# Down projections of two MLPs in 2x2 blocks: seven products instead of eight

## The chip, the cores and the metric

The kernel runs on one core of one Trainium2 chip. The metric is the device time in microseconds, the median of the timed runs.

## The reference

A decoder trunk of two layers over 512 tokens and a width of 1024, all in float32. Layer 0 begins with a mixer of a convolution and a state-space scan, layer 1 with gated linear attention; both go on with cross-attention into 256 memory tokens and an MLP. What bears on this case is the MLP and the layer norm behind it:

```
def sq_relu_mlp(x, w1, w2):          # w1 1024 x 4096, w2 4096 x 1024
    return jnp.square(jax.nn.relu(x @ w1)) @ w2
h = layer_norm(DEEPNORM_ALPHA * h + sq_relu_mlp(h, mlp_w1[i], mlp_w2[i]), ln_g[i, 2], ln_b[i, 2])
```

## The kernel before

**Products.** Every matrix product is made from pairs. `split` (L104, L105) turns a float32 tile into hi, its rounding to float32r, made by ScalarE, and lo, the exact rest, made by VectorE (or by GpSimd where `lo_pat` says "g"). `mm3` (L159 to L161) makes one product from three matmuls, hi x hi, hi x lo and lo x hi, each 128 by 128 by 512 columns. Weights come as blocks of 1 MB (tag "ws", two buffers, issued by SyncE) and are split in `wpair` into tiles of 128 x 1024 (tags "wh" and "wl", six buffers each).

**The MLP.** `mlp` works through the 4096 hidden features in four quarters (`qd`) of 1024. In the up part `feat_tiles` makes 8 tiles of 128 features x 512 tokens, 24 matmuls each, with the activations moving. The evacuation takes relu on ScalarE (L473), the square on VectorE (L475) and splits it at once. In the down part `tok_half` makes 512 output columns for four tiles of 128 tokens, twice; each token tile collects 8 feature tiles, 24 matmuls. VectorE adds the sums to the residual h (L485 in the first quarter, with the factor alpha, L487 after). The last quarter goes through `out_proj`: its second half takes one token tile after the other, so that the layer norm of a tile (statistics L279 and L285, the inverse root on GpSimd L266 and L267, then L290 and L291) and its transposes into the next `xT` (`transpose_in`) stand beside the next tile's matmuls. The norm of the last tile has no matmuls of its own quarter behind it.

**Memory.** Activations of both layers come from one pool of 31 tiles of 128 x 512 (tag "t2"), open from the first cross-attention to the end. PSUM has three tags: "acc" (3 banks), "aux" (3) and "acb" (2); `acc()` deals acc and acb out in turn.

**Order.** The program is written for a tile framework whose planner plays it through with its own costs when it is built, and puts the instructions of each engine in the order in which they come out there. So the order on an engine is not that of the text; but once built it is fixed, and each engine takes its queue in order. Pools limit how far an engine can run ahead. SyncE's loads are one such queue.

Of the kernel before, what the change touches and what calls it, by code (L numbers as in the profile page):

```python
# [8 lines left out]
F32 = mybir.dt.float32  # L9
F32R = mybir.dt.float32r  # L10
AF = mybir.ActivationFunctionType
ALU = mybir.AluOpType
AX = mybir.AxisListType

P = 128
D = 1024
S = 512
NT = S // P
NK = D // P
ML = 256  # L20
FF = 4096
DEPTH = 2
ALPHA = (2 * DEPTH) ** 0.25
# [6 lines left out]
class Trunk:  # L30
# [26 lines left out]

    # issue order only, on one engine
    def after(self, b, a):
# [40 lines left out]

    # hi is src rounded to float32r, lo the exact rest
    def split(self, src, hi, lo, eng=None):
# [3 lines left out]

    # the same from PSUM, without the vector engine
    def split_pool(self, ps, hi, lo):
# [4 lines left out]

# [1 line left out]
    def lo_engine(self):  # L115
# [39 lines left out]

# [1 line left out]
    def mm3(self, out, a, b, start, stop):  # L157
        nc = self.nc
        nc.tensor.matmul(out, a[0], b[0], start=start, stop=False)  # L159
        nc.tensor.matmul(out, a[0], b[1], start=False, stop=False)  # L160
        nc.tensor.matmul(out, a[1], b[0], start=False, stop=stop)  # L161

# [4 lines left out]

    # output features on partitions; the first `halves` tiles begin with the first half of the tokens
    def feat_tiles(self, w, c0, n, xT, evac, halves=0):
# [29 lines left out]

    # output tokens on partitions, 512 columns; xT: list of (hi, lo) by k  # L200
    def tok_half(self, w, r0, c0, xT, evac, t_outer=False, nt=NT, late=None, joint=None):
# [36 lines left out]

# [1 line left out]
    def new_xT(self):  # L240
# [28 lines left out]

# [1 line left out]
    def begin_ln(self, i, j):  # L271
# [23 lines left out]

    # projection back to the residual, then layer norm
    def out_proj(self, w, xT, h, i, j, scaled=False, mid=None):
# [28 lines left out]

# [1 line left out]
    def mem_T(self):  # L328
# [133 lines left out]

# [1 line left out]
    def mlp(self, i, h, xT):  # L464
        nc = self.nc
        w1, w2 = self.aps["mlp_w1"][i], self.aps["mlp_w2"][i]
        NQ = 4
        for qd in range(NQ):
            r2 = []

            def evac(m, ps):
                r = self.t2()
                nc.scalar.activation(r, ps, AF.Relu)  # L473
                sq = self.t2()
                nc.vector.tensor_tensor(sq, r, r, ALU.mult)  # L475
                hi, lo = self.t2(F32R), self.t2(F32R)
                self.split(sq, hi, lo)
                r2.append((hi, lo))
            self.feat_tiles(w1, qd * D, NK, xT, evac, halves=4 if qd == 0 else 0)
            if qd < NQ - 1:  # L480
                for hf in range(2):
                    def ev(t, ps, hf=hf):
                        y = h[t, hf]
                        if qd == 0:
                            nc.vector.scalar_tensor_tensor(y, y, ALPHA, ps, ALU.mult, ALU.add)  # L485
                        else:
                            nc.vector.tensor_tensor(y, y, ps, ALU.add)  # L487
                    self.tok_half(w2, qd * D, hf * S, r2, ev)
            else:
                return self.out_proj(w2[qd * D:(qd + 1) * D, :], r2, h, i, 2, scaled=True)  # L490

# [23 lines left out]
    def run(self):  # L515
        tc = self.tc
        self.kv_dram = [tc.dram_tile([2, 8, P, S], F32, name=f"kvd{i}") for i in range(DEPTH)]
        with tc.tile_pool(name="ep", bufs=8, reuse_waits="tile") as self.ep, self.sbuf_phase(16) as self.tp, \
                self.psum_phase(False) as self.px:
            self.lo_pat = "g"  # L520
            xT = self.load_x(self.aps["even_w_in"][0], D)
            h, xT = self.even(xT, self.x_tiles)
        self.lo_pat = "v"
        with tc.tile_pool(name="rp", bufs=4, reuse_waits="tile") as self.ep, self.sbuf_phase(31) as self.tp, \
                self.psum_phase(True) as self.px:
            h, xT = self.xa(0, h, xT, *self.kv_load(0))
            h, xT = self.mlp(0, h, xT)
            h, xT = self.odd(h, xT)
            h, xT = self.xa(1, h, xT, *self.kv_load(1))
            self.mlp(1, h, xT)  # L530

# [1 line left out]
    def bc(self, ap, n, w):  # L533
# [41 lines left out]

    # x times a [D, 16] weight, transposed: the sum of rows 0..15 and 32..47 of [P, S] in PSUM
    def narrow(self, w, c0, xT):
# [76 lines left out]

    # silu gate times two, from a product in PSUM
    def gate2(self, ps, th):
# [22 lines left out]
    def ssd_chunk(self, g, c, d, xs, BT, CT):  # L679
        nc = self.nc  # L680
        v = nc.vector
        r3 = lambda ap: ap.rearrange("p (h c) -> p h c", c=64)
        sl = slice(c * P, (c + 1) * P)
# [9 lines left out]
        pb = self.aux()  # L693
        nc.tensor.matmul(pb[:, 0:P], BT[:, sl], CT[:, sl], start=True, stop=True)
        cb = self.sp.tile([P, P], F32, tag="cb", bufs=2, name=self.nm("cb"))
        bt, xw = None, None
        if c < 3:
            nc.tensor.transpose(pb[:, P:2 * P], BT[:, sl], self.ident)
            bt = self.sp.tile([P, P], F32, tag="bt", bufs=2, name=self.nm("bt"))
            nc.scalar.copy(bt, pb[:, P:2 * P])  # L700
            xw = self.t2()
            nc.gpsimd.tensor_tensor(r3(xw), r3(xdt), self.bc(d["dte"][:, hs], 8, 64), ALU.mult)
# [4 lines left out]
        for q in range(2):  # L707
# [4 lines left out]
            for j in range(4):  # L712
                h = c * 16 + h0 + j
# [8 lines left out]
    def ssd_out(self, g, c, d, p, xs, CT, H, zs, norm_g):  # L722
        nc = self.nc
        v = nc.vector
        r3 = lambda ap: ap.rearrange("p (h c) -> p h c", c=64)
        sl = slice(c * P, (c + 1) * P)
# [3 lines left out]
        for i in range(8):  # L730
            last = nc.tensor.matmul(py[:, i * 64:(i + 1) * 64], Ms[i // 4][:, (i % 4) * P:(i % 4 + 1) * P],
                                    xdt[:, i * 64:(i + 1) * 64], start=True, stop=True)
# [7 lines left out]
        if c < 3:  # L740
            pst = self.aux()
            with self.tc.issue_after(last.ins):
                nc.tensor.matmul(pst, p["bt"], p["xw"], start=True, stop=True)
            H2 = self.sp.tile([P, S], F32, tag="H", bufs=2, name=self.nm("H"))
            if c == 0:
                nc.scalar.copy(H2, pst)
            else:
                nc.gpsimd.tensor_tensor(r3(H2), r3(H), self.bc(d["cd"][:, hs], 8, 64), ALU.mult)
                v.tensor_tensor(H2, H2, pst, ALU.add)
            H = H2  # L750
# [25 lines left out]

    # one tile of the wide conv, a tap at a time
    def conv_taps(self, u):
# [129 lines left out]

# [1 line left out]
    def odd(self, h, xT):  # L910
# [24 lines left out]

        # 16 x the log gate, summed within chunks of 64
        az, mn, bs = [], [], []
# [210 lines left out]
```

## Time and profile before

| what | value |
|---|---|
| timed runs | 1651.32, 1651.59, 1653.93 us, median 1651.59 |
| span of the profiled execution (its own time is not listed apart) | 1651.3 us |
| TensorE matmuls: busy, share | 1617.0 us, 98% |
| VectorE | 957.9 us, 58% |
| ScalarE | 614.0 us, 37% |
| GpSimd | 363.8 us, 22% |
| mean granted TensorE clock, share of full speed | 0.994 |

The profile is of one execution. Matmul records overlap, since matmuls are pipelined: what one costs is the distance between starts, not the length of its record. The MLP of layer 0 lies at some 553 to 900 us, that of layer 1 from some 1290 us to the end.

### The profile page before, as it was taken

What the parts mean: (1) busy time and instruction counts of PE and PEld (TensorE: products, weight loads), DVE (VectorE), ACT (ScalarE), POOL (GpSimd) and SP (SyncE); (2) the same over time, 40 slices, a digit from 0 to 9 for tenths busy, and PEclk for the clock granted to TensorE, in tenths of its full rate; (3) what the DMA queues carried; (4) which work ended last, traced back from release to release, by engine and by line L of the source; (5) the groups of instructions that cost most, each with busy time, mean ns of one, the idle gap of its engine ahead of it and who ended that gap; (6) DMA issues with size and microseconds to landing.
All of it is one profiled execution on the core that took longest, in us unless ns stands there. A gap on an engine that the chain in (4) does not pass through costs nothing.

```text
span 1651.3 us, 19881 instructions
## 1 busy us (share of the span) xinstructions
PE 1617.0 (98%) x8010; PEld 1353.9 (82%) x8010; DVE 957.9 (58%) x1279; ACT 614.0 (37%) x994; POOL 363.8 (22%) x288
## 2 busy tenths in 40 slices
PE   8998999999999999999999999999999999999998
PEld 7886878788988988888888788897988988888886
DVE  3998999975655634433447644444745734433445
ACT  4355557552442422323232534352332423223230
POOL 4654957744102100000001121222201200000001
PEclk9998999999999999999999999999999999999999
DMA  7224226632711332233232232275311322332221
GB/s 243 95 78 127 87 68 205 216 127 77 255 51 52 128 102 89 90 102 102 85 100 77 103 102 77 77 252 200 125 61 52 128 93 86 102 103 92 87 77 51
DMA packets 134798, 182.72 MB, mean 111 GB/s; under 512 B 6821, under 2 KB 83797, under 8 KB 134706
## 3 DMA queue, kind: packets, MB, share of 16 engines
q1 hardware_dynamic: 134162, 181.26, 33.5%
q8 instruction: 63, 1.03, 0.3%
q0 software_dynamic: 544, 0.20, 0.1%
q14 instruction: 29, 0.24, 0.0%
HBM read 170.92 MB, written 10.52 MB: 110 GB/s over the span
## 4 chain that ended last, share of the span: by engine, by line
PE 79%; DVE 14%; DMA 3%; issue 2%; POOL 1%; ACT 1%; SPq 0%; POOLq 0%; DVEq 0%; ACTq 0%
PE acc L161 16%; PE acc L159 16%; PE acc L160 16%; PE accb L161 9%; PE accb L159 9%; PE accb L160 9%; DVE cv L805 6%; DVE xs L651 1%; DMA ws<-in_odd_w_out_dram 1%; DVE h L291 1%; DMA kvd<-kv 1%; PE aux L253 1%; DVE t L651 1%; PE aux L161 1%; PE aux L159 1%
## 5 line engine op out<-in xcount | busy, mean ns | idle before, releaser
L105 DVE TENSOR_TENSOR wl<-ws,wh 128x1024 fp32r<-128x1024 f32 x216 | 271.7, 1260 | 430.0 <-ACT wh L104 430.0
L104 ACT CAST wh<-ws 128x1024 fp32r<-128x1024 f32 x276 | 288.9, 1050 | 560.5 <-PE acc L161 175.4
L159 PE MATMUL acc<-t,wh 128*128 128x512 f32 (+1 forms) x856 | 309.9, 363 | 6.0 <-DVE h L660 3.8
L161 PE MATMUL acc<-t,wl 128*128 128x512 f32 (+1 forms) x856 | 309.3, 362 | 0.0
L160 PE MATMUL acc<-t,wh 128*128 128x512 f32 (+1 forms) x856 | 309.2, 361 | 0.0
L159 PE MATMUL acc<-wh,t 128*128 128x512 f32 x704 | 279.0, 396 | 2.0 <-ACT kv L111 1.2
L160 PE MATMUL acc<-wl,t 128*128 128x512 f32 x704 | 278.5, 396 | 0.0
L161 PE MATMUL acc<-wh,t 128*128 128x512 f32 x704 | 276.0, 395 | 0.0
L105 POOL TENSOR_TENSOR wl<-ws,wh 128x1024 fp32r<-128x1024 f32 x60 | 151.3, 2531 | 300.0 <-ACT wh L104 299.6
L159 PEld LDWEIGHTS acc<-t,wh 128*128 128x128 f32 x856 | 163.7, 192 | 30.6 <-DVE h L660 4.0
L161 PEld LDWEIGHTS acc<-t,wl 128*128 128x128 f32 x856 | 163.8, 191 | 24.5 <-issue 1.7
L160 PEld LDWEIGHTS acc<-t,wh 128*128 128x128 f32 x856 | 164.0, 192 | 23.9 <-issue 1.0
L159 PEld LDWEIGHTS acc<-wh,t 128*128 128x128 f32 x704 | 132.5, 188 | 32.4 <-ACT kv L111 1.6
L160 PEld LDWEIGHTS acc<-wl,t 128*128 128x128 f32 x704 | 132.6, 188 | 29.9 <-issue 1.2
L161 PEld LDWEIGHTS acc<-wh,t 128*128 128x128 f32 x704 | 132.4, 188 | 29.4 <-issue 0.2
L805 DVE SCALAR_TENSOR_TENSOR cv<-u,cw,cv 128x511 f32<-128x511 f32 (+24 forms) x210 | 145.5, 728 | 0.5
L160 PE MATMUL accb<-wl,t 128*128 128x512 f32 x352 | 139.4, 396 | 0.0
L159 PE MATMUL accb<-wh,t 128*128 128x512 f32 x352 | 138.8, 394 | 0.0
L161 PE MATMUL accb<-wh,t 128*128 128x512 f32 x352 | 138.3, 395 | 0.0
L266 POOL TENSOR_SCALAR s<-s 128x1 f32<-128x1 f32 (+1 forms) x44 | 23.0, 524 | 474.5 <-DVE s L285 438.4
L161 PE MATMUL accb<-t,wl 128*128 128x512 f32 (+1 forms) x344 | 119.1, 346 | 0.0
L160 PE MATMUL accb<-t,wh 128*128 128x512 f32 (+1 forms) x344 | 118.9, 346 | 0.0
(286 smaller groups left out, 2135.5 us busy)
## 6 DMA issues: line engine op xcount, KB each, us to landing
ws<-in_mlp_w_dram SPq DMA_DIRECT2D x64, 1024.0 KB, 5.3
ws<-in_even_w_in_dram SPq DMA_DIRECT2D x17, 1024.0 KB, 5.3
ws<-in_odd_w_in_dram SPq DMA_DIRECT2D x12, 1024.0 KB, 5.1
ws<-in_xa_w_k_dram SPq DMA_DIRECT2D x8, 1024.0 KB, 5.0
ws<-in_xa_w_v_dram SPq DMA_DIRECT2D x8, 1024.0 KB, 6.0
kvd<-kv SPq DMA_DIRECT2D x32, 256.0 KB, 5.1
ws<-in_even_w_out_dram SPq DMA_DIRECT2D x8, 1024.0 KB, 5.2
ws<-in_xa_w_q_dram SPq DMA_DIRECT2D x8, 1024.0 KB, 5.9
```

Of the source, the lines that this page charges most:

```text
L104: self.last_hi = nc.scalar.copy(hi, src)
L105: (eng or nc.vector).tensor_tensor(lo, src, hi.bitcast(F32), ALU.subtract)
L159: nc.tensor.matmul(out, a[0], b[0], start=start, stop=False)
L160: nc.tensor.matmul(out, a[0], b[1], start=False, stop=False)
L161: nc.tensor.matmul(out, a[1], b[0], start=False, stop=stop)
L253: nc.tensor.transpose(ps[:, j * P:(j + 1) * P], halves[hf][:, j * P:(j + 1) * P], self.ident)
L266: nc.gpsimd.tensor_scalar(r, var, scale, eps, op0=ALU.mult, op1=ALU.add)
L291: nc.vector.scalar_tensor_tensor(y, y, r, ln["b"][:, sl], ALU.mult, ALU.add)
L651: nc.vector.scalar_tensor_tensor(c[:, s:], x[:, :S - s], w[:, 3 - s:4 - s], c[:, s:], ALU.mult, ALU.add)
L805: nc.vector.scalar_tensor_tensor(cs[j][:, s:], u[m][:, :S - s], w[:, 30 - s:31 - s], cs[j][:, s:], ALU.mult, ALU.add)
```

## The change

The down projection of each quarter becomes one call of `strassen`. The activations of the quarter (512 tokens x 1024 features) are cut into 2 x 2 blocks of 256 tokens x 512 features, the weights (1024 x 1024) into 2 x 2 blocks of 512 x 512, and the four output blocks come from seven block products, P1 to P7, in Winograd's form. With A11 and A12 the two feature halves of the first 256 tokens (`A1`, `A2` at `t0`), A21 and A22 those of the last 256 (`t1`):

```
P1 = A11 B11              P2 = A12 B21
P3 = (A21 + A22)(B12 - B11)
P4 = (A21 + A22 - A11)(B22 - B12 + B11)
P5 = (A12 - A21 - A22 + A11) B22
P6 = (A11 - A21)(B22 - B12)
P7 = A22 (B22 - B12 + B11 - B21)
```

Each product is 2 token tiles x 4 feature tiles x 3 matmuls. P2 goes on in the banks of P1, P5 in those of P3, P7 in those of P6, after VectorE has read what stood there. P1 + P4 is needed in three output blocks; it is collected in `E` over all four quarters and added once, in the last. Sums and differences of blocks are made by VectorE, in float32, before the split; each of the seven operand pairs is split on its own. The squared activations stay unsplit in tiles of four features ("ab"); the square moves to ScalarE. Two up tiles of the next quarter stand ahead of each call but the last. The layer norm of token tiles 0 and 1 comes with P5, that of tiles 2 and 3 with P7. The down weights get buffers of their own ("sq", four). The pool of activations is opened once per layer and closed before the MLP, which opens its own (`mp`) in the same memory. The scratch memory of DMAs is cut to 4096 bytes, and three tags of the state-space scan change pools. Blank lines and lost comments are left out here.

```
-    def mm3(self, out, a, b, start, stop):
-        nc = self.nc
-        nc.tensor.matmul(out, a[0], b[0], start=start, stop=False)
-        nc.tensor.matmul(out, a[0], b[1], start=False, stop=False)
-        nc.tensor.matmul(out, a[1], b[0], start=False, stop=stop)
+
+
+    def mm3(self, out, a, b, start, stop, more=False):
+        nc = self.nc
+        nc.tensor.matmul(out, a[0], b[0], start=start, stop=False, skip_group_check=more)
+        nc.tensor.matmul(out, a[0], b[1], start=False, stop=False, skip_group_check=more)
+        nc.tensor.matmul(out, a[1], b[0], start=False, stop=stop, skip_group_check=more)
...
+    def blk_load(self, w, r, c):
+        st = self.mp.tile([P, 4, S], F32, tag="sq", bufs=4, name=self.nm("sq"))
+        self.nc.sync.dma_start(st, w[r:r + S, c:c + S].rearrange("(k p) c -> p k c", p=P))
+        return st
+    def blk_w(self, st):
+        r = []
+        for j in range(2):
+            hi, lo = self.wpair(st[:, 2 * j:2 * j + 2, :], (P, 2, S))
+            r += [(hi[:, i, :], lo[:, i, :]) for i in range(2)]
+        return r
+    def blk_a(self, src):
+        hi, lo = [self.mp.tile([P, 4, 256], F32R, tag=t, bufs=3, name=self.nm(t)) for t in ("sh", "sl")]
+        self.split(src, hi, lo)
+        return hi, lo
+    def blk_sub(self, dst, a, b):
+        for j in range(2):
+            ks = slice(2 * j, 2 * j + 2)
+            self.nc.vector.tensor_tensor(dst[:, ks, :], a[:, ks, :], b[:, ks, :], ALU.subtract)
+    def blk_prod(self, pss, a, w, start, evac):
+        for i in range(2):
+            sl = slice(i * P, (i + 1) * P)
+            for k in range(4):
+                self.mm3(pss[i], (a[0][:, k, sl], a[1][:, k, sl]), w[k], start and k == 0, k == 3, not start)
+            evac(i, pss[i])
+    def strassen(self, w, r0, A, h, E, first, ln=None, mid=None):
+        nc = self.nc
+        v = nc.vector
+        A1, A2 = A
+        t0, t1 = slice(0, 256), slice(256, 512)
+        X = self.blk_load(w, r0, 0)
+        B21 = self.blk_load(w, r0 + S, 0)
+        B12 = self.blk_load(w, r0, S)
+        B22 = self.blk_load(w, r0 + S, S)
+        def add(t, hf, begin):
+            def f(i, ps):
+                y = h[t + i, hf]
+                if begin and first:
+                    v.scalar_tensor_tensor(y, y, ALPHA, ps, ALU.mult, ALU.add)
+                else:
+                    v.tensor_tensor(y, y, ps, ALU.add)
+            return f
+        def e1(i, ps):
+            if first:
+                nc.scalar.copy(E[i], ps)
+            else:
+                v.tensor_tensor(E[i], E[i], ps, ALU.add)
+        def done(t, hf, begin):
+            f = add(t, hf, begin)
+            def g(i, ps):
+                f(i, ps)
+                if ln is not None:
+                    self.ln_half(ln, t + i, hf, h[t + i, hf])
+            return g
+        pa = [self.ps.tile([P, S], F32, tag="acc", name=self.nm("acc")) for _ in range(2)]
+        self.blk_prod(pa, self.blk_a(A1[:, :, t0]), self.blk_w(X), True, e1)
+        self.blk_prod(pa, self.blk_a(A2[:, :, t0]), self.blk_w(B21), False, done(0, 0, True))
+        self.blk_sub(X, B12, X)
+        Sx = self.mp.tile([P, 4, 256], F32, tag="sx", bufs=2, name=self.nm("sx"))
+        v.tensor_tensor(Sx, A1[:, :, t1], A2[:, :, t1], ALU.add)
+        pc = [self.accb() for _ in range(2)]
+        self.blk_prod(pc, self.blk_a(Sx), self.blk_w(X), True, add(2, 1, True))
+        self.blk_sub(X, B22, X)
+        v.tensor_tensor(Sx, Sx, A1[:, :, t0], ALU.subtract)
+        pb = [self.aux() for _ in range(2)]
+        def e2(i, ps):
+            v.tensor_tensor(E[i], E[i], ps, ALU.add)
+            if ln is not None:
+                for y in (h[i, 1], h[2 + i, 1], h[2 + i, 0]):
+                    v.tensor_tensor(y, y, E[i], ALU.add)
+        self.blk_prod(pb, self.blk_a(Sx), self.blk_w(X), True, e2)
+        self.blk_sub(B12, B22, B12)
+        v.tensor_tensor(Sx, A2[:, :, t0], Sx, ALU.subtract)
+        v.tensor_tensor(A1[:, :, t1], A1[:, :, t0], A1[:, :, t1], ALU.subtract)
+        def c12(i, ps):
+            done(0, 1, True)(i, ps)
+            if ln is not None:
+                self.ln_finish(ln, i)
+        self.blk_prod(pc, self.blk_a(Sx), self.blk_w(B22), False, c12)
+        self.blk_sub(X, B21, X)
+        pd = [self.ps.tile([P, S], F32, tag="acc", name=self.nm("acc")) for _ in range(2)]
+        self.blk_prod(pd, self.blk_a(A1[:, :, t1]), self.blk_w(B12), True, done(2, 1, False))
+        if mid is not None:
+            mid()
+        def c21(i, ps):
+            done(2, 0, True)(i, ps)
+            if ln is not None:
+                self.ln_finish(ln, 2 + i)
+        self.blk_prod(pd, self.blk_a(A2[:, :, t1]), self.blk_w(X), False, c21)
     def mlp(self, i, h, xT):
         nc = self.nc
         w1, w2 = self.aps["mlp_w1"][i], self.aps["mlp_w2"][i]
         NQ = 4
+        A = {}
+        def up(qd, m0, n, halves=0):
+            def evac(j, ps):
+                m = m0 + j
+                if m % 4 == 0:
+                    A[qd, m // 4] = self.mp.tile([P, 4, S], F32, tag="ab", bufs=3, name=self.nm("ab"))
+                r = A[qd, m // 4][:, m % 4, :]
+                nc.scalar.activation(r, ps, AF.Relu)
+                nc.scalar.activation(r, r, AF.Square)
+            self.feat_tiles(w1, qd * D + m0 * P, n, xT, evac, halves=halves)
+        E = [self.mp.tile([P, S], F32, tag="E", bufs=2, name=self.nm("E")) for _ in range(2)]
+        up(0, 0, NK, halves=4)
         for qd in range(NQ):
-            r2 = []
-
-            def evac(m, ps):
-                r = self.t2()
-                nc.scalar.activation(r, ps, AF.Relu)
-                sq = self.t2()
-                nc.vector.tensor_tensor(sq, r, r, ALU.mult)
-                hi, lo = self.t2(F32R), self.t2(F32R)
-                self.split(sq, hi, lo)
-                r2.append((hi, lo))
-            self.feat_tiles(w1, qd * D, NK, xT, evac, halves=4 if qd == 0 else 0)
-            if qd < NQ - 1:
-                for hf in range(2):
-                    def ev(t, ps, hf=hf):
-                        y = h[t, hf]
-                        if qd == 0:
-                            nc.vector.scalar_tensor_tensor(y, y, ALPHA, ps, ALU.mult, ALU.add)
-                        else:
-                            nc.vector.tensor_tensor(y, y, ps, ALU.add)
-                    self.tok_half(w2, qd * D, hf * S, r2, ev)
-            else:
-                return self.out_proj(w2[qd * D:(qd + 1) * D, :], r2, h, i, 2, scaled=True)
+            last = qd == NQ - 1
+            if not last:
+                up(qd + 1, 0, 2)
+                self.strassen(w2, qd * D, [A[qd, 0], A[qd, 1]], h, E, qd == 0)
+                up(qd + 1, 2, NK - 2)
+        ln = self.begin_ln(i, 2)
+        nxt = None
+        if not ln["out"]:
+            nxt = self.new_xT()
+            ln["xt"] = self.xT_tiles
+        def late(t):
+            if not ln["out"]:
+                self.transpose_in(t, [ln["h"][t, 0], ln["h"][t, 1]], ln["xt"])
+        def mid():
+            for t in range(2):
+                late(t)
+        self.strassen(w2, (NQ - 1) * D, [A[NQ - 1, 0], A[NQ - 1, 1]], h, E, False, ln, mid)
+        for t in range(2, NT):
+            self.pending.append(lambda t=t: late(t))
+        return ln["h"], nxt
...
-        with tc.tile_pool(name="rp", bufs=4, reuse_waits="tile") as self.ep, self.sbuf_phase(31) as self.tp, \
-                self.psum_phase(True) as self.px:
-            h, xT = self.xa(0, h, xT, *self.kv_load(0))
-            h, xT = self.mlp(0, h, xT)
-            h, xT = self.odd(h, xT)
-            h, xT = self.xa(1, h, xT, *self.kv_load(1))
-            self.mlp(1, h, xT)
-    # ---- layer-0 mixer: conv module and SSD ----
+        with self.psum_phase(True) as self.px:
+            for i in range(DEPTH):
+                with tc.tile_pool(name=self.nm("rp"), bufs=4, reuse_waits="tile") as self.ep, self.sbuf_phase(31) as self.tp:
+                    if i == 1:
+                        h, xT = self.odd(h, xT)
+                    h, xT = self.xa(i, h, xT, *self.kv_load(i))
+                with tc.tile_pool(name=self.nm("mp"), bufs=2, reuse_waits="tile") as self.mp:
+                    h, xT = self.mlp(i, h, xT)
...
-        cb = self.sp.tile([P, P], F32, tag="cb", bufs=2, name=self.nm("cb"))
+        cb = self.ep.tile([P, P], F32, tag="cb", bufs=2, name=self.nm("cb"))
-            bt = self.sp.tile([P, P], F32, tag="bt", bufs=2, name=self.nm("bt"))
+            bt = self.ep.tile([P, P], F32, tag="bt", bufs=2, name=self.nm("bt"))
-            H2 = self.sp.tile([P, S], F32, tag="H", bufs=2, name=self.nm("H"))
+            H2 = self.ep.tile([P, S], F32, tag="H", bufs=2, name=self.nm("H"))
...
-    nc = _bacc.Bacc("TRN2", target_bir_lowering=False, num_devices=1)
+    nc = _bacc.Bacc("TRN2", target_bir_lowering=False, num_devices=1, dynamic_dma_scratch_size=4096)
```

## Rows read from the trace of the kernel before

**Rows 1.** The page: span; busy us of each engine, share, instructions.
```profile
span 1651.3 us, 19881 instructions
...
PE 1617.0 (98%) x8010; PEld 1353.9 (82%) x8010; DVE 957.9 (58%) x1279; ACT 614.0 (37%) x994; POOL 363.8 (22%) x288
```

**Rows 2.** Stages: length, busy us of each engine, granted clock, DMA share, GB/s.
```profile
core 0: us, PE busy (x) PEld busy (x) DVE busy (x) ACT busy (x) POOL busy (x), PEclk, DMA share, GB/s
...
697.00:785.00 88.00, 88.00 (x385) 72.09 (x384) 35.47 (x40) 25.73 (x32) 0.00 (x0) 1.00 0.30 96
...
881.00:905.00 24.00, 24.00 (x118) 19.80 (x117) 20.44 (x30) 7.25 (x10) 5.05 (x6) 1.00 0.19 57
...
1355.00:1443.00 88.00, 88.00 (x385) 72.10 (x384) 35.30 (x41) 25.73 (x32) 0.00 (x0) 1.00 0.29 96
```

**Rows 3.** The page: the chain that ended last, by engine and line.
```profile
PE acc L161 16%; PE acc L159 16%; PE acc L160 16%; PE accb L161 9%; PE accb L159 9%; PE accb L160 9%; DVE cv L805 6%; DVE xs L651 1%; DMA ws<-in_odd_w_out_dram 1%; DVE h L291 1%; DMA kvd<-kv 1%; PE aux L253 1%; DVE t L651 1%; PE aux L161 1%; PE aux L159 1%
```

**Rows 4.** VectorE in order of time, layer 0's MLP: start, length, line.
```profile
606.83 1.23 DVE L105 TENSOR_TENSOR wl<-ws,wh 128x1024 fp32r<-128x1024 f32 x1 [4.35 <-ACT wh L104]
609.19 1.38 DVE L485 SCALAR_TENSOR_TENSOR h<-h,acc 128x512 f32<-128x512 f32 x2 [1.13 <-PE acc L161]
...
631.50 0.69 DVE L485 SCALAR_TENSOR_TENSOR h<-h,accb 128x512 f32<-128x512 f32 x1 [1.19 <-PE accb L161]
...
646.54 0.68 DVE L475 TENSOR_TENSOR t<-t 128x512 f32<-128x512 f32 x1
...
651.97 0.69 DVE L475 TENSOR_TENSOR t<-t 128x512 f32<-128x512 f32 x1
...
697.35 0.69 DVE L487 TENSOR_TENSOR h<-h,acc 128x512 f32<-128x512 f32 x1 [1.13 <-PE acc L161]
```

**Rows 5.** VectorE in order of time at the end of layer 1's MLP.
```profile
1637.74 0.69 DVE L308 TENSOR_TENSOR h<-h,accb 128x512 f32<-128x512 f32 x1 [0.61 <-PE accb L161]
...
1643.33 0.69 DVE L308 TENSOR_TENSOR h<-h,acc 128x512 f32<-128x512 f32 x1 [0.62 <-PE acc L161]
...
1644.78 0.21 DVE L285 BATCH_NORM_AGGREGATE s<-s 128x2 f32<-128x12 f32 x1
1645.02 1.41 DVE L290 SCALAR_TENSOR_TENSOR h<-h,s,lng 128x512 f32<-128x512 f32 x2
1646.87 1.41 DVE L291 SCALAR_TENSOR_TENSOR h<-h,s,lnb 128x512 f32<-128x512 f32 x2 [0.44 <-POOL s L267]
```

**Rows 6.** VectorE's groups in layer 0's MLP: busy, mean ns, idle before.
```profile
L105 DVE TENSOR_TENSOR wl<-ws,wh 128x1024 fp32r<-128x1024 f32 x65 | 79.5, 1224 | 156.9 <-ACT wh L104 156.9
...
L475 DVE TENSOR_TENSOR t<-t 128x512 f32<-128x512 f32 x32 | 21.9, 684 | 0.0
L487 DVE TENSOR_TENSOR h<-h,acc 128x512 f32<-128x512 f32 x9 | 6.2, 689 | 3.6 <-PE acc L161 3.5
```

**Rows 7.** VectorE in order of time: two low parts back to back.
```profile
900.07 2.35 DVE L105 TENSOR_TENSOR wl<-ws,wh 128x1024 fp32r<-128x1024 f32 x2
```

**Rows 8.** ScalarE's groups over the whole span, shapes apart.
```profile
L104 ACT CAST wh<-ws 128x1024 fp32r<-128x1024 f32 x276 | 288.9, 1050 | 560.5 <-PE acc L161 175.4 <-PE acc L160 134.8 <-PE accb L161 119.7
...
L753 ACT ACTIVATE t<-t 128x512 f32<-128x512 f32 x8 | 5.1, 633 | 12.8 <-DVE t L751 12.8
```

**Rows 9.** TensorE in order of time at the end of layer 0's MLP.
```profile
902.61 1.04 PE L253 MATMUL aux<-ident,h 128*128 128x128 f32 x8
```

**Rows 10.** The page: DMA issues, KB each, median us to landing.
```profile
ws<-in_mlp_w_dram SPq DMA_DIRECT2D x64, 1024.0 KB, 5.3
```

**Rows 11.** Busy time and granted clock in layer 0's mixer.
```profile
140.00:145.00 5.00, 1.90 (x8) 1.74 (x9) 5.00 (x7) 3.22 (x5) 1.57 (x1) 0.84 0.00 0
145.00:150.00 5.00, 2.79 (x8) 1.78 (x8) 5.00 (x6) 0.75 (x3) 2.43 (x2) 0.50 0.60 189
150.00:155.00 5.00, 5.00 (x17) 3.92 (x17) 3.79 (x6) 3.56 (x8) 2.49 (x2) 0.63 0.89 230
```

**Rows 12.** GpSimd in order of time at the start.
```profile
29.27 9.48 POOL L105 TENSOR_TENSOR wl<-ws,wh 128x1024 fp32r<-128x1024 f32 x4 [14.94 <-ACT wh L104]
```

## The prediction

> **What bounds the kernel now.** I read the page's busy table first, then the busy time by stage, then the chain of waits, then the VectorE rows inside one MLP. TensorE is busy 1617.0 of 1651.3 us, VectorE 957.9, ScalarE 614.0 [rows 1]. By stage, both MLPs are pure TensorE: in 697 to 785 and again in 1355 to 1443 us TensorE is busy 88.00 of 88.00 us at granted clock 1.00 (the 2.4 GHz level), while VectorE works 35.5 us and ScalarE 25.7 us [rows 2]. The chain of waits has 75% of the span on the three lines of `mm3` alone (three times 16% and three times 9%) [rows 3]. So in the MLPs a matmul taken away is time taken away, as long as the two other engines, idle for 60% there, keep up.
>
> The timed median is 1651.59 us, 0.3 us above the span of the profiled execution; its own time is not listed apart from its span, and the lowest timed run (1651.32) equals it. I sum against 1651.3 and carry 0.3 over.
>
> **What goes.** One quarter of a layer's MLP has 192 matmuls up and 192 down. The quarter's period is 697.35 - 609.19 = 88.16 us between equal evacuations; the two down halves' evacuations lie 631.50 - 609.19 = 22.31 us apart, 96 matmuls, 232 ns each; the up tiles come every 651.97 - 646.54 = 5.43 us, 226 ns each [rows 4]. A block product is 2 token tiles x 4 feature tiles x 3 = 24 matmuls with activations stationary and weights moving, as in the old down half. The one place where 24 such matmuls stay in one bank, as they nearly do in the new code, is the last half of layer 1: evacuations at 1637.74 and 1643.33, again 5.58 us per 24 (1643.33 - 1637.74 = 5.59) [rows 5]. So the order within a product should not matter. Seven products for eight take away 24 matmuls, 5.58 us per quarter, and with 8 quarters **44.6 us**. The down part of a quarter becomes 7 x 5.58 = 39.1 us.
>
> The Trainium skill (TensorE: Matmul & The Clock Gate, "Back-to-back issue gap") gives about 131 ns as the sustained spacing of 512-column matmuls. By that the 192 matmuls would be worth an estimated 25.2 us and the sum below would turn slower than before. The trace disagrees: 232 ns here, at full clock, so I price with the rows.
>
> **What comes: VectorE.** A 128x1024 subtraction with both operands in SBUF is 1.22 us alone [rows 6] and 1.14 us behind another (two in 2.35) [rows 7]. The new f32 block subtractions and strided splits are not in the trace; the bounds are 1.14 and 1.37 (two of the 128x512 products at 0.684 [rows 6]); I take 1.14 in a full queue, since the nearest row has the same size. Per quarter: 14 weight low parts, 7 activation low parts, 8 block subtractions (4 subs in two pieces), 4 sums of activation blocks: 33 x 1.14 = 37.6 us. Evacuations: 14 x 0.69 [rows 6] = 9.7 us. Together 47.3 us in a stage of 39.1 us TensorE. Gone from the up part are the square (0.684) and the low part of each of 8 feature tiles. The up part keeps 8 weight low parts, 9.8 us, within 43.5 us. Over the quarter VectorE has 57 of 82.6 us. On the average it fits; inside the down part it does not, so what counts is how far it works ahead.
>
> ScalarE: 25.7 us per quarter now [rows 2]; 6 more weight casts and 7 activation casts of 128x1024 at 1.05 add 13.7, eight squares at 0.63 (the only square out of SBUF in the rows, which also sums) 5.0 [rows 8]: 44.4 of 82.6 us, with the old casts of the squares not even taken off. Hidden, cost 0.
>
> **Middle quarters (6).** The weight pools hold 6 pairs, three products' worth, and the activation pairs also three. Between the end of a quarter's up part and the first matmul of P7 TensorE has two tiles of the next quarter (10.9) and six products (33.5): 44.4 us. VectorE must do in it 47.3 - 1.4 (P7's own evacuations) + 2.3 (two weights of the next up tiles) = 48.2, less what was done before in its idle time. P1's three low parts, B21's two and the first block subtraction (two) can be, 7 x 1.14 = 8.0. That leaves 40.2 for 44.4: **0 us**. If nothing were done ahead, 3.8 us of stall plus 2.3 for the weights behind P7: 6 us per quarter. That the order is planned so that low parts go ahead of evacuations is seen before: the low part at 606.83 stands ahead of the evacuation at 609.19 [rows 4].
>
> **Last quarter (2).** Here nothing follows to fill TensorE, and no up tile stands between the last feature tile and P1, so A2 is ready only when P1 begins. What can have been done: 6 weight low parts (the buffers), one activation low part, 3 of the 4 block subtractions (6 pieces): 13 of 33. Left: 20 x 1.14 = 22.8. Then 12 evacuations of P1 to P6 (8.3), 6 additions of E (4.1), 6 statistics (4.1), and the layer norm of token tiles 0 and 1, 0.21 + 1.42 + 0.44 wait + 1.41 = 3.5 each [rows 5], 7.0. Sum 46.3, begun some 1.2 us after P1 (relu and square of the last tile, each about the square's 0.63). P7 could start at 47.5; TensorE is ready for it at 33.5. Stall 14.0 us per layer. With the layer norm put behind P7's operands it is 7; with the block subtractions not done ahead 21. I take 13, near the 14 worked out, since part of the norm can slip behind: **+26 us** for both layers (14 to 42).
>
> **Ends.** Now the last token tile's norm takes 1643.33 to 1648.28, 5.0 us, alone [rows 5]. After the change tiles 2 and 3 finish 2.8 us apart and share VectorE: two times 4.5 us of work begun 2.8 us before the last matmul ends, 6.2 us: **+1.3**. In layer 0 the same tail goes ahead of the mixer of layer 1. Today TensorE runs on through it (24.00 of 24.00 us in 881 to 905 [rows 2]; the last tile's transposes run at 902.61 [rows 9], inside that stretch, between matmuls of the next projection), and it still has token tiles 0 and 1 of that projection, 48 matmuls, 11 us, as cover for 6.2 us of norm, 4 splits of the transposes (2.7) and the transposes themselves (1.0). But the mixer's small loads now lie in memory that the MLP frees late, and a load takes some 5 us [rows 10]: **+2** (0 to 6). The loads themselves stay at 8 blocks of 1 MB per quarter, 96 GB/s [rows 2], with four buffers more: 0.
>
> **Clock.** In 140 to 145 us, with VectorE full and TensorE idle for over half, the granted clock is 0.84, in the 5 us after it 0.50 (the 1.2 GHz level), then 0.63 [rows 11]. Lost: 0.16 x 1.90 + 0.50 x 2.79 + 0.37 x 5.00 = 3.5 us for one such stretch. The stalls above are alike, but slower matmuls hide partly in a VectorE-bound stretch: **+2** for both layers (0 to 14).
>
> The smaller DMA scratch touches GpSimd's constant loads at the start; GpSimd is idle for 14.94 us between them and its first low part [rows 12], which covers some waits among them: 0.
>
> Sum: 1651.3 - 44.6 + 0 + 26 + 1.3 + 2 + 2 = 1638.0, plus 0.3: **1638 us**, 13 us faster.
>
> **Rivals.** (1) The planner puts the layer norm behind P7's operands and the ends stay covered: stalls 14 instead of 26, no loss at the ends or by the clock: 1651.6 - 44.6 + 14 + 1.3 = 1622. For it: VectorE's order is already by readiness; against: the norm stands ahead of P7 in the program.
> (2) Slower: the lead is used up in the middle quarters too. One mechanism: VectorE takes its queue in order, and an evacuation that waits for TensorE holds the next product's splits behind it; P7 and the next up weights come late by the 6 us worked out above, in six quarters: 1638 + 36 = 1674. It decides from 13.3 / 6 = 2.2 us of stall per middle quarter on. For it: 47.3 us of work on 39.1; against: VectorE's 60% idle time before it.
> (3) The clock falls in each of two stalls per layer and nothing hides it: 4 x 3.5 = 14 for the 2 above: 1650, no change. The same page of the Trainium skill ("Loop structure matters more than you think") says that idle stretches between bursts of matmuls throw TensorE to half rate. The trace agrees [rows 11], though it shows this beside full VectorE work and not in the MLPs.
> That seven products do not stand for eight would leave the time at 1651.6 plus the stalls; the count of matmuls tells at once, and I give it nothing.
>
> **Chances.** Forecast 0.50, (1) 0.20, (3) 0.08, (2) 0.22. What a measurement of this kernel can tell from no change is about 0.2%, 3.3 us. (1) and the forecast are faster, (3) is split, (2) is slower: faster 0.73, same 0.05, slower 0.22. The forecast's own range is 1621 (stalls 14, other terms at their low ends, some 1.3 us kept) to 1650; for 8 in 10 I add the lower half of (2): 1617 to 1662.
>
> **What would show it.** 7818 matmuls for 8010; middle quarters of 82.6 us with TensorE full; two stretches of some 13 us with VectorE full and TensorE waiting for low parts in P5 to P7 of each last quarter, and a granted clock under 1 there; VectorE at some 1130 us busy. I am wrong if TensorE idles in the middle quarters, or if a product takes other than 5.58 us.

## The result, and the profile after

The changed kernel takes 1635.15 us (median; 1634.73 to 1635.69 in 4 runs) against 1651.53: ratio 0.9896, 95% interval 0.9882 to 0.991, 16.4 us faster. The forecast was 1638 us, 13 us faster.

The page of the changed kernel, its first lines, to be held against [rows 1]:

```profile
span 1633.4 us, 19755 instructions
PE 1581.4 (97%) x7818; PEld 1321.2 (81%) x7818; DVE 1131.7 (69%) x1407; ACT 722.8 (44%) x1102; POOL 361.8 (22%) x288
```

The matmuls are the 7818 that were to be there, VectorE has 174 us more work, and the span is 17.9 us shorter. (Each later timed execution lies 1.7 us above its own span. So the span of 1651.3 before belongs, by an estimate from that, to an execution of some 1653 us, near the slowest timed one of 1653.93, and the spans show about 1.5 us more gain than the times.)

Busy time by stage in the changed kernel, columns as in [rows 2]: one middle quarter, then the last quarter of layer 0 in steps of 10 us, then that of layer 1:

```profile
705.00:787.00 82.00, 82.00 (x359) 67.19 (x358) 56.10 (x55) 38.42 (x45) 0.00 (x0) 1.00 0.32 101
...
845.00:855.00 10.00, 9.65 (x42) 7.49 (x40) 10.00 (x12) 4.95 (x5) 0.00 (x0) 1.00 0.00 1
855.00:865.00 10.00, 7.04 (x28) 5.03 (x28) 10.00 (x13) 4.55 (x5) 0.00 (x0) 1.00 0.01 2
865.00:875.00 10.00, 7.61 (x26) 6.09 (x27) 8.84 (x12) 1.44 (x2) 0.95 (x1) 0.83 0.00 0
875.00:885.00 10.00, 9.09 (x40) 7.02 (x38) 9.85 (x15) 3.15 (x3) 2.81 (x5) 1.00 0.43 124
885.00:895.00 10.00, 6.62 (x23) 4.16 (x24) 9.94 (x19) 3.49 (x6) 0.00 (x0) 0.66 0.75 218
...
1583.00:1593.00 10.00, 8.71 (x38) 6.74 (x36) 10.00 (x12) 4.95 (x5) 0.00 (x0) 1.00 0.01 2
1593.00:1603.00 10.00, 7.42 (x28) 5.49 (x28) 10.00 (x12) 4.94 (x5) 0.00 (x0) 0.93 0.00 0
1603.00:1613.00 10.00, 7.87 (x22) 5.89 (x21) 9.24 (x14) 0.00 (x0) 0.90 (x2) 0.56 0.00 0
```

In the middle quarter TensorE is full at full clock, with VectorE at 56 of 82 us. In the last quarters VectorE is full, TensorE idles (10.0 us between 845 and 895, 6.0 us between 1583 and 1613), and the granted clock falls: by the 10 us rows, TensorE runs at the 1.2 GHz level for some 3.4 + 6.8 us in layer 0 and 1.4 + 8.8 us in layer 1 (an estimate: the rows' means taken as a mix of the two levels).

VectorE in order of time: P4's addition to E, second token tile, in the second and the third quarter of layer 0:

```profile
706.77 0.68 DVE L549 TENSOR_TENSOR E<-E,aux 128x512 f32<-128x512 f32 x1
...
789.38 0.68 DVE L549 TENSOR_TENSOR E<-E,aux 128x512 f32<-128x512 f32 x1
```

A quarter now takes 82.61 us, 5.55 less than the 88.16 of [rows 4].

Where TensorE waited in layer 0's last quarter (in brackets the idle time and what ended it), and VectorE's queue there:

```profile
856.38 0.50 PE L162 MATMUL aux<-wh,sl 128*128 128x512 f32 x1 [1.73 <-DVE sl L105]
...
862.60 0.50 PE L160 MATMUL accb<-wh,sh 128*128 128x512 f32 x1 [1.32 <-ACT sh L104]
...
867.39 0.61 PE L162 MATMUL accb<-wh,sl 128*128 128x512 f32 x1 [2.65 <-DVE sl L105]
...
886.47 1.32 PE L254 MATMUL aux<-ident,h 128*128 128x128 f32 x8 [2.38 <-DVE h L292]
```

```profile
860.25 1.22 DVE L555 TENSOR_TENSOR sx<-ab,sx 128x1024 f32<-128x1024 f32 x1
861.39 0.69 DVE L280 BATCH_NORM_STATS2 s<-h 128x6 f32<-128x512 f32 x1
861.99 0.68 DVE L549 TENSOR_TENSOR E<-E,aux 128x512 f32<-128x512 f32 x1
862.58 1.23 DVE L105 TENSOR_TENSOR wl<-sq,wh 128x1024 fp32r<-128x1024 f32 x1
863.71 0.69 DVE L549 TENSOR_TENSOR E<-E,aux 128x512 f32<-128x512 f32 x1
864.31 1.90 DVE L552 TENSOR_TENSOR h<-h,E 128x512 f32<-128x512 f32 x3
866.12 1.22 DVE L105 TENSOR_TENSOR sl<-sx,sh 128x1024 fp32r<-128x1024 f32 x1
867.25 1.23 DVE L105 TENSOR_TENSOR sl<-ab,sh 128x1024 fp32r<-128x1024 f32 x1
868.39 1.90 DVE L552 TENSOR_TENSOR h<-h,E 128x512 f32<-128x512 f32 x3
870.19 1.23 DVE L105 TENSOR_TENSOR sl<-ab,sh 128x1024 fp32r<-128x1024 f32 x1
871.33 1.22 DVE L105 TENSOR_TENSOR wl<-sq,wh 128x1024 fp32r<-128x1024 f32 x1
...
880.70 1.40 DVE L291 SCALAR_TENSOR_TENSOR h<-h,s,lng 128x512 f32<-128x512 f32 x2
```

The first three waits, 5.7 us, are for P4's and P5's activations (bank tags aux and accb), not for P7's; the other 4.3 us are at the hand-over to layer 1, the longest of them for the layer norm. Ahead of P5's low part (866.12) stand three additions of E to the residual (L552, 864.31), which P5 does not need. P7's last low part is made at 871.33 and the layer norm of the first token tiles only at 880.70: the planner put the norm behind P7's operands.

In layer 1 the first wait is the same (1.74 us); the other two, a cast on ScalarE ahead of the first of these, and the granted clock between them, are:

```profile
1600.47 0.50 PE L160 MATMUL accb<-wh,sh 128*128 128x512 f32 x1 [2.12 <-ACT sh L104]
...
1605.60 0.80 PE L162 MATMUL accb<-wh,sl 128*128 128x512 f32 x1 [2.13 <-DVE sl L105]
```

```profile
1598.43 1.04 ACT L104 CAST wh<-sq 128x1024 fp32r<-128x1024 f32 x1 [0.33 <-PE aux L162]
```

```profile
1601.00:1603.50 2.50, 2.46 (x7) 1.31 (x6) 2.50 (x4) 1.32 (x2) 0.00 (x0) 0.60 0.00 0
```

Here the clock is down before the third wait begins, and the second wait is 0.8 us longer than in layer 0: on ScalarE a second weight cast, the one shown, stands ahead of P5's activation cast.

The tail of layer 1, to be held against [rows 5], is 6.8 us from the last matmul's end (1623.5) instead of 5.0:

```profile
1623.57 0.69 DVE L518 TENSOR_TENSOR h<-h,acc 128x512 f32<-128x512 f32 x1 [1.14 <-PE acc L162]
...
1628.94 1.41 DVE L292 SCALAR_TENSOR_TENSOR h<-h,s,lnb 128x512 f32<-128x512 f32 x2
```

For the experiments, stage lengths in the traces (us). Layer 0 runs from the first maximum of its softmax to the first gate matmul of layer 1, so it holds the MLP and the hand-over; layer 1 from its last softmax maximum to the end of the last matmul; the tail from there to the end of VectorE's last step.

| kernel | layer 0 | layer 1 | tail | median time |
|---|---|---|---|---|
| before | 478.3 | 405.9 | 5.0 | 1651.53 |
| changed | 469.8 | 394.0 | 6.8 | 1635.15 |
| last quarter with eight products (e2) | 462.2 | 389.2 | 5.0 | 1617.45 |
| no lead (e3) | 484.7 | 403.8 | 8.0 | 1662.61 |
| additions of E left out (e4) | 462.1 | 388.4 | 6.8 | 1621.23 |
| additions of E on GpSimd (e6) | 465.5 | 392.4 | 6.8 | 1629.51 |
| additions of E and block subtractions on GpSimd (e5) | 467.5 | 392.7 | 6.8 | 1630.04 |
| additions of E late (e7) | 466.6 | 388.6 | 10.2 | 1628.54 |

### The profile page after: what moved, and what is told of

The parts are those of the page before. It is cut to its first block, busy times and chain, and to the rows that moved or that the text cites. A ratio compares the mean times of both kernels' runs of the same rounds, so it can differ in the third digit from the quotient of the medians.

```text
span 1633.4 us, 19755 instructions
## 1 busy us (share of the span) xinstructions
PE 1581.4 (97%) x7818; PEld 1321.2 (81%) x7818; DVE 1131.7 (69%) x1407; ACT 722.8 (44%) x1102; POOL 361.8 (22%) x288
## 4 chain that ended last, share of the span: by engine, by line
PE 75%; DVE 19%; issue 2%; DMA 1%; POOL 1%; ACT 1%; SPq 0%; DVEq 0%; POOLq 0%; ACTq 0%
PE acc L162 15%; PE acc L160 15%; PE acc L161 15%; PE accb L162 8%; PE accb L160 8%; PE accb L161 8%; DVE cv L930 7%; DVE wl L105 2%; DVE xs L776 1%; PE aux L160 1%; PE aux L162 1%; PE aux L161 1%; DVE h L292 1%; PE aux L254 1%; DVE t L776 1%
## 5 line engine op out<-in xcount | busy, mean ns | idle before, releaser
L104 ACT CAST wh<-ws 128x1024 fp32r<-128x1024 f32 x212 | 221.9, 1050 | 326.1 <-PE acc L162 128.1
L105 DVE TENSOR_TENSOR wl<-ws,wh 128x1024 fp32r<-128x1024 f32 x152 | 193.4, 1274 | 175.9 <-ACT wh L104 175.6
L105 DVE TENSOR_TENSOR wl<-sq,wh 128x1024 fp32r<-128x1024 f32 x112 | 136.2, 1222 | 105.1 <-ACT wh L104 105.1
L104 ACT CAST wh<-sq 128x1024 fp32r<-128x1024 f32 x112 | 116.6, 1048 | 203.7 <-PE acc L161 66.8
L160 PE MATMUL acc<-wh,t 128*128 128x512 f32 x416 | 165.8, 399 | 1.5 <-ACT t L104 1.2
L161 PE MATMUL acc<-wl,t 128*128 128x512 f32 x416 | 164.9, 396 | 0.0
L162 PE MATMUL acc<-wh,t 128*128 128x512 f32 x416 | 163.0, 397 | 0.0
L160 PE MATMUL accb<-t,wh 128*128 128x512 f32 (+1 forms) x352 | 122.0, 347 | 0.0
L161 PE MATMUL accb<-t,wh 128*128 128x512 f32 (+1 forms) x352 | 121.9, 346 | 0.0
L104 ACT CAST t<-aux 128x512 fp32r<-128x512 f32 (+1 forms) x84 | 44.9, 548 | 139.9 <-PE aux L254 114.1
L160 PE MATMUL acc<-wh,sh 128*128 128x512 f32 x256 | 101.6, 397 | 0.0
L161 PE MATMUL acc<-wl,sh 128*128 128x512 f32 x256 | 101.5, 396 | 0.0
```

Source lines behind the costliest of these rows:

```text
L104: self.last_hi = nc.scalar.copy(hi, src)
L105: (eng or nc.vector).tensor_tensor(lo, src, hi.bitcast(F32), ALU.subtract)
L160: nc.tensor.matmul(out, a[0], b[0], start=start, stop=False, skip_group_check=more)
L161: nc.tensor.matmul(out, a[0], b[1], start=False, stop=False, skip_group_check=more)
L162: nc.tensor.matmul(out, a[1], b[0], start=False, stop=stop, skip_group_check=more)
```

## The experiments

**e1: the squares alone.** In the kernel before:

```
-                nc.vector.tensor_tensor(sq, r, r, ALU.mult)
+                nc.scalar.activation(sq, r, AF.Square)
...
+    ... dynamic_dma_scratch_size=4096
```

> The kernel before with the square moved to ScalarE and the DMA scratch cut, nothing else. Theory A (the gain is the matmuls taken away, all the rest of the change costs or gives nothing by itself): TensorE is full in the MLPs before and after, so 1651.5 within 3 us. Rival (the square taken off VectorE is worth time): over 3 us faster.

Measured: 1651.39 us, ratio 1.0002 (0.9993 to 1.0011). A middle quarter, columns as in [rows 2]:

```profile
697.00:785.00 88.00, 88.00 (x385) 72.10 (x384) 30.64 (x32) 30.82 (x40) 0.00 (x0) 1.00 0.30 96
```

Five microseconds of VectorE work went to ScalarE and TensorE stayed at 88.00 of 88.00. Theory A: the squares and the scratch memory, changed together, are worth no time.

**e2: the last quarter with eight products.** In the changed kernel:

```
+        def part(m):            # hi and lo of one squared feature tile, in "sq" buffers
+            self.split(A[NQ - 1, m // 4][:, m % 4, :], hi, lo)
...
-        self.strassen(w2, (NQ - 1) * D, [A[NQ - 1, 0], A[NQ - 1, 1]], h, E, False, ln, mid)
+        return self.out_proj(w2[(NQ - 1) * D:, :], r2, h, i, 2, scaled=True)
```

> The changed kernel with the last quarter of each layer done with eight products again, in the old way; P1 + P4 is added to the residual after the third quarter. Theory A (each middle quarter gives its 5.58 us whole, the last quarter loses more by VectorE work, idle TensorE and a halved clock than its 5.58): 1651.5 - 6 x 5.58 = 1618, within 3 us, TensorE full in both MLPs at granted clock 1.00, and the old tail of 5.0 us. Rival (the loss lies elsewhere: the memory of the MLP shared with the mixers, the middle quarters, the start): 1635 - 11 by the two products given back is not won, 1635 to 1646.

Measured: 1617.45 us (1616.88 to 1617.84), ratio 0.9793 (0.978 to 0.9806), 33.8 us faster than the kernel before in the same round; 33.5 were expected. Layer 0 is 16.1 and layer 1 16.7 us shorter than before; three times 5.58 is 16.7. The last quarters of both layers:

```profile
835.00:885.00 50.00, 50.00 (x230) 40.88 (x229) 30.48 (x43) 10.96 (x14) 6.48 (x8) 1.00 0.23 69
...
1528.00:1573.00 45.00, 45.00 (x198) 36.93 (x197) 18.31 (x20) 19.96 (x27) 0.00 (x0) 1.00 0.31 100
```

TensorE is full at full clock and VectorE has time left. Theory A: six middle quarters give all they promised, and the last quarter, which should have given 11.2 us more, costs 17.7 instead. The MLP and the mixers share memory here too, and layer 0 is within 0.7 us of what three quarters promise, so the shared memory costs at most that here. This is the fastest version of the study.

**e3: no lead.** In the changed kernel:

```
-                up(qd + 1, 0, 2)
                 self.strassen(w2, qd * D, [A[qd, 0], A[qd, 1]], h, E, qd == 0)
-                up(qd + 1, 2, NK - 2)
+                up(qd + 1, 0, NK)
```

> The changed kernel without the two up tiles ahead of each middle quarter's seven products: all eight stand behind. So A2 is ready only when P1 begins, as in the last quarter, but additions of E, statistics and norm are not there. Theory A (it is the extra VectorE work that stalls the last quarter): what is left for VectorE before P7 is 20 x 1.14 + 12 x 0.69 + 1.2 = 32.3 us against 33.5 on TensorE, so at most 2 us per middle quarter, 1635 to 1647, with gaps of under 1 us each. Rival (the missing lead stalls it): each of six middle quarters idles as the last does, 6 to 10 us, and the clock falls: 1671 to 1695.

Measured: 1662.61 us, ratio 1.0065 (1.0051 to 1.0078): slower than before the change, 27.5 us behind the changed kernel, 4.6 for each of six middle quarters if all of it is put down to them, between the two expectations. Of this, 18.2 us are TensorE's idle time in the six (3.0 each), 1.2 us a longer tail; in three of the six the granted clock also fell to 0.83 over 10 us. P4's second addition to E in three quarters of layer 0, and the longest of the waits in the second:

```profile
614.62 0.67 DVE L549 TENSOR_TENSOR E<-E,aux 128x512 f32<-128x512 f32 x1
...
703.13 0.68 DVE L549 TENSOR_TENSOR E<-E,aux 128x512 f32<-128x512 f32 x1
...
789.30 0.68 DVE L549 TENSOR_TENSOR E<-E,aux 128x512 f32<-128x512 f32 x1
```

```profile
702.61 0.50 PE L160 MATMUL accb<-wh,sh 128*128 128x512 f32 x1 [1.29 <-ACT sh L104]
```

The quarters take 88.5 and 86.2 us, nearly as long as with eight products (88.16). My bound of 2 us was wrong because it asked only whether VectorE is through by P7. The waits stand at P4 and P5 again, each for the cast or the low part of an activation sum: the sums for P3, P4 and P5 are made one from the other, the first needs A2, and each shares VectorE's queue with evacuations and weight low parts. There is a time by which each product must be served, and the early ones miss it though the sum until P7 fits. So the lead of two up tiles is worth 27 us. Without it a middle quarter idles 3.0 us, about half of the 5.7 and 6.0 us in the last quarters' products, so the missing lead explains about half of that stall; no run gave the last quarter a lead.

One more reading: the edit does not touch layer 1's last quarter. Its waits are 1.73, 1.32 and 2.64 us, as in layer 0 of the changed kernel, yet the granted clock stays at 1.00:

```profile
1634.07 0.50 PE L162 MATMUL accb<-wh,sl 128*128 128x512 f32 x1 [2.64 <-DVE sl L105]
```

```profile
1634.00:1644.00 10.00, 9.93 (x43) 8.07 (x44) 10.00 (x17) 0.00 (x0) 1.43 (x4) 1.00 0.00 0
```

So the length of the waits alone does not settle whether the clock falls.

**e4: the additions of E left out.** In the changed kernel:

```
-            if ln is not None:
-                for y in (h[i, 1], h[2 + i, 1], h[2 + i, 0]):
-                    v.tensor_tensor(y, y, E[i], ALU.add)
```

> The changed kernel without the six additions of E (P1 + P4) to the residual in the last quarter of each layer: this part of the result is left out. Theory A (TensorE waits for VectorE's queue there): 6 x 0.69 = 4.1 us of queue go, just ahead of the third gap; TensorE's idle time in the last quarter falls by 3 to 4 us per layer and some of the half clock with it: 1624 to 1630. Rival (the gaps come from the late A2, or from the order of the products, not from the amount of VectorE work): 1635 within 2 us.

Measured: 1621.23 us, ratio 0.9816 (0.9802 to 0.9829), 13.9 us better than the changed kernel, more than the 5 to 11 expected. Layer 0's last quarter, and the third wait:

```profile
855.00:865.00 10.00, 7.07 (x28) 5.04 (x28) 10.00 (x11) 4.81 (x5) 0.00 (x0) 1.00 0.01 2
865.00:875.00 10.00, 9.63 (x41) 7.50 (x41) 9.69 (x15) 2.24 (x4) 2.26 (x5) 1.00 0.00 0
```

```profile
865.32 0.50 PE L162 MATMUL accb<-wh,sl 128*128 128x512 f32 x1 [0.84 <-DVE sl L105]
```

The first two waits stay (1.73 and 1.30 us), the third falls from 2.65 to 0.84, and the clock stays at 1.00. TensorE's idle time falls from 10.0 to 5.4 us in layer 0 and from 6.0 to 3.9 in layer 1, 6.7 in all; the other half of the gain fits the clock, which no longer falls. More than half of layer 0's share, 2.8 us, is won at the hand-over: the norm that began at 880.70 now begins some 9 us earlier:

```profile
871.62 1.40 DVE L291 SCALAR_TENSOR_TENSOR h<-h,s,lng 128x512 f32<-128x512 f32 x2
```

Both theories hold a part: the first two waits of layer 0 stay without the additions and fit the late A2; of the third, 1.8 us are theirs. In layer 1 the second wait falls as well, from 2.12 to 1.29 us, since ScalarE's planned order changed with the edit and P5's cast follows the first weight cast at once:

```profile
1589.66 1.04 ACT L104 CAST sh<-sx 128x1024 fp32r<-128x1024 f32 x1 [0.47 <-DVE sx L552]
```

So part of this gain is order, and the run does not price the amount of VectorE's work alone.

**e6 and e5: GpSimd helps.** In the changed kernel (e5 also gives `blk_sub` of B22 - B12 and of P7's block to GpSimd in the last quarter):

```
-                    v.tensor_tensor(y, y, E[i], ALU.add)
+                    nc.gpsimd.tensor_tensor(y, y, E[i], ALU.add)
```

> The changed kernel with the six additions of E in the last quarter made by GpSimd, which has nothing to do there. Theory A with free engines (VectorE's queue is the limit and GpSimd works beside it): the same 4.1 us leave VectorE's queue as when the additions were left out (1621.2), so 1621 to 1625, granted clock 1.00 in the last quarter. Rival (the two engines get in each other's way: before the change a VectorE step at 538.18 took 2.88 us instead of 0.74 beside a GpSimd subtraction): GpSimd's 128x512 steps are 1.29 to 1.53 us long in the rows; VectorE loses up to that for each, 6 x 1.4 = 8.4 for the 4.1 taken off: 1635 to 1645.

> As the one before, and of the last quarter's four block subtractions the last two (B22 - B12 and the one for P7) also on GpSimd, four steps of some 2.5 us. Theory A with free engines: VectorE's queue loses 4 x 1.14 = 4.6 us more per layer, but of these only what was not done ahead counts: 1616 to 1622. Rival (in each other's way): VectorE loses 4 x 2.5 = 10 us for 4.6: later than with the additions alone, 1640 to 1655.

Measured: e6 1629.51 us, ratio 0.9856 (0.9838 to 0.9874); e5 1630.04 us, ratio 0.9859 (0.984 to 0.9877). Neither expectation: 5.6 us better than the changed kernel, 8.3 worse than with the additions left out, and the block subtractions give nothing. GpSimd and VectorE in e6, layer 1:

```profile
1595.27 12.39 POOL L552 TENSOR_TENSOR h<-h,E 128x512 f32<-128x512 f32 x6 [311.37 <-DVE E L549]
```

```profile
1598.49 4.54 DVE L105 TENSOR_TENSOR sl<-ab,sh 128x1024 fp32r<-128x1024 f32 x2
1602.95 2.31 DVE L105 TENSOR_TENSOR wl<-sq,wh 128x1024 fp32r<-128x1024 f32 x1
```

While GpSimd adds, a low part takes VectorE 2.3 us instead of 1.2, and one of GpSimd's additions up to 2.28 us, where its shortest takes 1.29. The two take turns: of GpSimd's six additions five take 2.2 us or more, and the last, when VectorE has no low part left, 1.29. The Trainium skill (SBUF — State Buffer, "SBUF: two separate sides") says that a VectorE instruction with two SBUF inputs and a GpSimd instruction hold a common port one after the other, each for its whole length; these rows agree. What was won is the place in the queue: P5's low part no longer stands behind the additions, and the third wait is 1.34 us in both layers. But a new wait comes ahead of P7, for VectorE's evacuation of P6, here in layer 0 (1.84 us in layer 1):

```profile
879.31 0.47 PE L160 MATMUL acc<-wh,sh 128*128 128x512 f32 x1 [2.95 <-DVE h L518]
```

So TensorE's idle time is 15.0 us in all, hardly less than the 16.0 of the changed kernel. The gain goes with the clock: 1.00 through layer 0's last quarter, and 0.83 in one row of 10 us in layer 1.

**e7: the additions of E late.** In the changed kernel, instead of six additions behind P4, one in each block's own evacuation behind P5, P6 and P7:

```
                 f(i, ps)
                 if ln is not None:
+                    if (t, hf) != (0, 0):
+                        v.tensor_tensor(h[t + i, hf], h[t + i, hf], E[i], ALU.add)
```

> The changed kernel with the six additions of E still on VectorE, but each made where its block is finished (behind P5, P6 and P7) instead of all six right behind P4. Theory A, refined (what counts is what stands in VectorE's queue ahead of P5's operands, and the half clock that the third gap sets off): the third gap falls from 2.6 us to 0.8 as when the additions were left out, the clock stays at 1.00 there, and some of the 4.1 us per layer comes back later as norm and tail: 1621.2 plus up to 3, 1621 to 1627. Rival (the amount of VectorE work up to the end of the layer sets the time, wherever it stands): 1635 within 3 us.

Measured: 1628.54 us (1628.00 to 1632.01), ratio 0.9865 (0.9849 to 0.9882): 1.5 us above the expected range, and the median 3.5 us below the rival's. The third wait in layer 0 and a new one at the hand-over, then VectorE's last step:

```profile
863.99 0.50 PE L162 MATMUL accb<-wh,sl 128*128 128x512 f32 x1 [0.83 <-DVE sl L105]
...
884.99 1.03 PE L254 MATMUL aux<-ident,h 128*128 128x128 f32 x4 [3.67 <-DVE h L292]
```

```profile
1619.94 2.74 DVE L292 SCALAR_TENSOR_TENSOR h<-h,s,lnb 128x512 f32<-128x512 f32 x4
```

The third wait is 0.83 us as in e4, and layer 1 up to the last matmul is as short as there (388.6 against 388.4). But the work comes back where nothing covers it: the tail is 10.2 us instead of 6.8, and in layer 0 the transposes wait 3.67 us for the norm, and the clock falls to 0.83 over the 10 us behind it. So moving the same work gains 6.6 us and leaving it out 13.9: place counts for about half. I had set the tail and the hand-over too low.

## Why the prediction was right, step by step

**What goes: right.** 44.6 us of matmuls: the middle quarters' period shows 5.55 us each, and e2 gave 33.8 us for six.

**Middle quarters, 0 us: right, by a thinner reason than given.** TensorE is full there. But e3 shows that a balance up to P7 does not prove it; what covers is the lead.

**Last quarter, +26 us, and clock, +2: the sum was near, both terms were off.** The layers lost 22.3 - 8.5 = 13.8 and 22.3 - 11.8 = 10.5 us, 24.3 in all. Of this 16.0 is TensorE idle: 11.7 in the last quarters' products, 4.3 at the hand-over. The rest, 8.3, I put down mainly to the half clock; in e4, with the clock at 1.00, the loss beyond the idle time is still 0.7 and 1.0 us, so the clock's own share is nearer 6.6. The step that was off is the place of the stall: I put it ahead of P7 and counted the layer norm before it. The norm went behind P7's operands, as rival (1) had it, which takes 7 us off per layer; the waits stood at P4 and P5 and came to 5.7 and 6.0 us, not 13. The clock price per stall (3.5 us) was near the 3 to 4 us per layer here, but I let most of it hide.

**Ends: +1.3 for the tail, 1.8 measured; +2 for the hand-over, 4.3 measured.** TensorE idles there (2.38 + 0.75 + 0.68 + 0.47) for the norm and the transposes of tiles 0 and 1, not for the mixer's loads as I had thought: the norm that went behind P7's operands comes late here.

So the range and the sign rest on sound steps, but the nearness of 1638 to 1635 partly on luck: 14 us too much stall stand against some 5 us too little clock and 2 us too little hand-over.

**Rival (1)** had the order of the norm right and the stall near (14 for 11.7). It missed the time, 1622, because it put the ends and the clock at no loss. **Rival (2)** did not come about. Without the lead (e3) the middle quarters do stall, but at P4 and P5 and not at P7. **Rival (3)** had the clock fall in both layers right; its 14 us for it are about twice what the clock cost.

## What to carry to other kernels

Work that saves the full engine's time and loads another paid here where that other engine had a lead of independent work, and not where it had none: done in six of eight places, this change gives 33.8 us, in all eight 16.4. Test the queue of the helping engine against each product's own due time, not against the end of the stage. In a stretch where TensorE already waits a little, microseconds of helper work can cost nearly double, since the clock can go too.

## What the runs showed of the hardware that I had not expected

Six VectorE steps per layer, 1.90 us for three and 7.6 us in both layers, cost 13.9 us of time (changed kernel against e4). Short waits can be followed by a lower granted clock, but not always: after 1.73, 1.32 and 2.65 us it was 0.83 in 865 to 875, after nearly the same waits in layer 1 of e3 1.00, and a longer wait of 2.95 us in layer 0 of e6 left it at 1.00. What decides is open. GpSimd is no free helper beside a VectorE that reads two operands from SBUF: 2.3 us for a low part instead of 1.2 (e6).
